# Block 2's gate and up in 512- and 256-column passes with its taps on ScalarE and GpSimd, and a fifth three-pass chunk in the first feed-forward

## The chip, the cores and the metric

The kernel runs on one core of a Trainium2 chip. The metric is the device time of one execution in microseconds (us). The engines are named as the profile names them: PE (TensorE, the matrix multiplier), PEld (its weight loads, which run beside the matmuls), DVE (VectorE), ACT (ScalarE), POOL (GpSimd) and SP (the engine that issues most of the loads). Every engine works through its own instructions in the order in which they were written; an instruction that waits holds up all that stand behind it on its engine.

## What is computed

A sequence of 256 positions by 1024 channels goes through two layers of a hybrid block (feed-forward, mixing of pooling and attention, feed-forward), and then through one layer of a second block ("block 2"), which ends in a feed-forward whose gate passes a causal convolution of three taps. Feed-forwards are five in all, each with 2816 hidden channels. All arithmetic is held to float32 accuracy.

```python
def swiglu(h, w_gate_up, w_down):             # the four of the two-layer block
    a, b = jnp.split(h @ w_gate_up, 2, axis=-1)
    return (jax.nn.silu(a) * b) @ w_down

def causal_dwconv(x, w, b):
    K = w.shape[0]
    S = x.shape[1]
    xp = jnp.pad(x, ((0, 0), (K - 1, 0), (0, 0)))
    y = xp[:, 0:S] * w[0]
    for k in range(1, K):
        y = y + xp[:, k:k + S] * w[k]
    return y + b
```

In block 2's feed-forward the gate is `gelu(causal_dwconv(h @ w_gate))` in place of the silu, and the layer's output is the sequence plus the down projection of gate times up. Ahead of every feed-forward stands a root-mean-square norm: each position is multiplied by its own factor (called RS here) and each channel by a gain.

## The kernel before

Channels lie on the 128 partitions and the 256 positions on the free axis, so the sequence `xT` is 8 tiles of 128x256. PE multiplies float32 numbers in a cut format, so every operand is split in a high part and a low one: ACT copies the raw weight to its high part (`wh`, line 86), DVE subtracts that from the raw weight and leaves the low part (`wl`, line 160); activations are split in the same way into the two halves of a tile `ahl`. Three products of the parts are summed: low by high, high by low, high by high.

A feed-forward has 22 hidden tiles, numbered k. Gate and up run in 11 chunks j of two hidden tiles each: a chunk is four column tiles (gate and up of k = 2j, then gate and up of k = 2j + 1), each with 8 weight tiles of 128x128, so 32 weight tiles a chunk. The down projection is 8 rows of 22 weight tiles. Two forms of the product are in use:

- **three-pass** (`cols`, `col_part`, `mm3`, lines 201 to 203): three matmuls of 256 columns for each weight tile. Its result lies in one half of a PSUM bank. The activations carry the gain and not RS, so the result is multiplied by RS when it is read.
- **wide** (`wide_cols`, `passes`, lines 247 and 252): for a group of weight tiles first a matmul of 512 columns each (the weight's high part against both halves of `ahl`), then one of 256 columns each (its low part against the high half). The result fills a whole bank, and DVE sums the two halves (`sum_halves`, line 255). Its activations carry gain and RS: `weigh` makes them, one call for each of the 8 tiles (DVE line 441, ACT line 86, POOL line 446, which subtracts the high part to leave the low one).

RS comes out of the norm's sums only while the first chunk is being multiplied, so a feed-forward begins in three-pass form. Each of the four silu feed-forwards runs three chunks so, the very first four (its first two in a form of their own, `opening`), makes the weighed activations in the last two of these, and runs the other chunks wide. Block 2's feed-forward (`gate is conv_gate`) runs all 11 chunks three-pass; it does not weigh anything and multiplies by RS on DVE where the gate is read (line 500) and where the down projection's result is read (line 457 in `add_to_x`). Down is wide in all five, but for its last row, which is three-pass.

After a column tile, `emit` or `halves` starts the gate, and `defer(n, f)` writes the later steps n ticks on; a tick is one group of matmuls. This, with `split` (which writes the weights' splits between ticks), fixes the order on every engine. The gate of block 2 (`conv_gate`) is an Identity with the third tap as scale and the bias (ACT, line 559), two taps by DVE (lines 562 and 563), and a Gelu (ACT, line 565). `finish` multiplies by up and splits the product for the down projection: copy on ACT (line 86, `ahl<-hh`), subtraction on POOL (line 512). Its multiplication is on POOL (line 513) in the silu feed-forwards, on DVE from PSUM in block 2. `silu_gate` is one ACT instruction (line 553). PSUM has four banks for these products, tag `mm`; the 128x256 work tiles share six buffers (`wt`), the larger activations 35 (`ut`).

Of the kernel before, what the change touches and what calls it, by code (L numbers as in the profile page):

```python
# [8 lines left out]
F = mybir.dt.float32  # L9
R = mybir.dt.float32r  # L10
AF = mybir.ActivationFunctionType
OP = mybir.AluOpType
AX = mybir.AxisListType

P = 128
S = 256
# [3 lines left out]
FT = DFF // P  # L20
# [25 lines left out]
def drain(gen, plan={}):  # L46

    for n, _ in enumerate(gen):
        if n in plan:
            plan[n]()  # L50
# [3 lines left out]
def tile_hybrid_stack(ctx, tc, wts, cst, prm, rows, small, out, x):  # L54
    nc = tc.nc
    pool = lambda name, bufs, **kw: ctx.enter_context(tc.tile_pool(name=name, bufs=bufs, **kw))
    cp = pool("consts", 1)
    wp = pool("weights", 4)
    up = pool("acts", 35)
    sp = pool("work", 2)  # L60
    mm = pool("mm", 4, space=bass.MemoryType.PSUM)
    tpp = pool("tp", 2, space=bass.MemoryType.PSUM)
# [5 lines left out]
        return up.tile(shape, dt, tag="u", name=name)  # L68

    def wt(name):  # L70
        return sp.tile([P, S], F, tag="w", name=name, bufs=6)

    def tiny(n, name, bufs=2):
        return sp.tile([P, n], F, tag=name, name=name, bufs=bufs)
# [10 lines left out]
    def copy(dst, src, **kw):  # L85
        nc.scalar.activation(dst, src, AF.Copy, **kw)  # L86
# [82 lines left out]
    def defer(steps, f):  # L169
        heapq.heappush(tasks, (now[0] + steps, next(order), f))  # L170
# [219 lines left out]
    RS = {}  # L390
# [58 lines left out]
    def add_to_x(norm, scale, rb=None):  # L449
        def emit(j, ps):  # L450
            if len(ps.shape) == 3 or rb is not None:
                d = wt("dx")
                if len(ps.shape) == 3:
                    sum_halves(d, ps)
                    ps = d
                if rb is not None:
                    nc.vector.tensor_tensor(d, ps, rb, OP.mult)
                ps = d
            nc.vector.scalar_tensor_tensor(xT[:, j], ps, scale, xT[:, j], op0=OP.mult, op1=OP.add)  # L459
            if norm is None:  # L460
                nc.sync.dma_start(out[:, j], xT[:, j])
            else:
                norm.done(j)
        return emit
# [25 lines left out]
    def feed_forward(norm, gate, nxt, scale, first=False, beside=None):  # L490


        hT = Acts(True)
        pace[0] = 2

        def emit(j):
            def f(i, pg, pu, both=None):
                k = 2 * j + i
                z, v = wt("sl"), wt("hh")
                nc.vector.tensor_tensor(z, pg, RS["bc"], OP.mult)  # L500
                if gate is not conv_gate:
                    nc.vector.tensor_tensor(v, pu, RS["bc"], OP.mult)
                a, n = gate(k, z)
                finish(k, v, a, n, pu if gate is conv_gate else v)
            return f

        def finish(k, v, a, n, src):
            eng = nc.gpsimd if src is v else nc.vector
            def last():
                dh, dl = hT.get(k)  # L510
                copy(dh, v)
                nc.gpsimd.tensor_tensor(dl, v, dh.bitcast(F), OP.subtract)  # L512
            defer(n, lambda: eng.tensor_tensor(v, src, a, OP.mult))  # L513
            defer(n + 1, last)

        def halves(j):

            gated = []

            def f(i, ps):  # L520
                k = 2 * j + i // 2
                z = wt("hh" if i % 2 else "sl")
                sum_halves(z, ps)
                if i % 2 == 0:
                    gated.append(gate(k, z))
                else:
                    a, n = gated.pop()
                    finish(k, z, a, max(n - 3, 1), z)
            return f
        if beside is not None:  # L530
            defer(60, beside)
        if first:
            opening(norm, emit(0), emit(1))
        done = 2 if first else 0
        if gate is conv_gate:
            last, factor = 11, RS
        else:
            last, factor = 4 if first else 3, {"bc": None}
        for j in range(done, last):
            plan = {}  # L540
            if last < 11 and j >= last - 2:
                steps = (0, 2, 4, 6) if j == last - 2 else (0, 1, 3, 4)
                plan = {m: lambda n=n: norm.weigh(4 * (j - last + 2) + n) for n, m in enumerate(steps)}
            drain(cols(norm.acts, KT, emit(j), None if j else norm), plan)
        pace[0], lead[0] = 1, 0
        for j in range(last, 11):
            drain(wide_cols(norm.weighed, halves(j)))
        flush()
        pace[0], lead[0] = 2, 1
        drain(wide_rows(hT, FT, *[add_to_x(nxt, scale, factor["bc"])] * 2))  # L550

    def silu_gate(f, z):
        defer(1, lambda: nc.scalar.activation(z, z, AF.Silu))
# [2 lines left out]
    def conv_gate(f, z):  # L556
        w = lambda k: pr[:, P_FCW + 3 * f + k:P_FCW + 3 * f + k + 1]
        a = wt("cz")
        nc.scalar.activation(a, z, AF.Identity, scale=w(2), bias=pr[:, P_FCB + f:P_FCB + f + 1])

        def rest():
            nc.vector.scalar_tensor_tensor(a[:, 1:], z[:, :S - 1], w(1), a[:, 1:], op0=OP.mult, op1=OP.add)
            nc.vector.scalar_tensor_tensor(a[:, 2:], z[:, :S - 2], w(0), a[:, 2:], op0=OP.mult, op1=OP.add)
        defer(1, rest)
        defer(2, lambda: nc.scalar.activation(a, a, AF.Gelu))
        return a, 3


    def rope_tables(col, rcol, n, name):
# [797 lines left out]
    norm = Norm(P_L, True)  # L1367
# [7 lines left out]
    for l in range(2):  # L1375
# [12 lines left out]
        norm = nxt  # L1388
# [140 lines left out]
```

## Time and profile before

| | before |
|---|---|
| time, median of 3 runs | 1494.89 us (1492.75 to 1497.18) |
| the profiled execution, its own time | 1496.27 us |
| its span | 1494.5 us |
| mean granted clock of PE | 0.995 of full speed |
| PE busy | 1466.1 us (98%), 10016 matmuls |
| DVE / ACT / POOL busy | 1043.8 / 772.8 / 442.3 us |

The span is the time from the first to the last instruction of the profiled execution; 1.8 us of its time lie around it. Shares of busy time are means over stages that differ. Where the chain of work runs through PE without a gap, only what PE does, or a new wait of PE, changes the time; where it leaves PE, the engine that it goes to counts. Block 2's feed-forward is at the end of the span, from about 1300 us on.

### The profile page before, as it was taken

How to read it: one execution, taken by the hardware profiler on the slowest of the kernel's cores; microseconds unless marked ns; L12 is line 12 of the kernel's file. 1: busy time of each engine (PE TensorE's matmuls, PEld its weight loads, DVE VectorE, ACT ScalarE, POOL GpSimd, SP SyncE). 2: the span in 40 equal slices, each digit the busy share in tenths (PEclk: the TensorE clock that was granted, in tenths of full speed). 3: DMA queues.
4: the chain of work that ended last, by engine and by line, in shares of the span. 5: the costliest groups of instructions: out<-in, count | busy, mean ns of one | idle time of the engine just before them, and what ended most of it. 6: DMA issues, size and time to landing. Idle time of an engine off the chain costs nothing.

```text
span 1494.5 us, 25193 instructions
## 1 busy us (share of the span) xinstructions
PE 1466.1 (98%) x10016; PEld 1351.9 (90%) x10016; DVE 1043.8 (70%) x1594; ACT 772.8 (52%) x1365; POOL 442.3 (30%) x513
## 2 busy tenths in 40 slices
PE   7999999999999999999999999999999799999998
PEld 7888888999988899888889999888987799999998
DVE  6867658577776757767586687676586666877673
ACT  4645335565554445544455645454376656555551
POOL 3642146013523135231360046322125101421200
PEclk9999999999999999999999999999999999999999
DMA  7555644445555544555443445546443533555561
GB/s 280 177 190 172 224 148 179 161 142 196 170 183 201 207 170 170 187 199 211 172 169 124 164 179 189 193 169 226 157 164 119 167 120 125 182 178 190 193 215 43
DMA packets 38710, 261.68 MB, mean 175 GB/s; under 512 B 4288, under 2 KB 5824, under 8 KB 7744
## 3 DMA queue, kind: packets, MB, share of 16 engines
q1 hardware_dynamic: 38016, 259.09, 49.5%
q8 instruction: 78, 1.28, 0.3%
q10 hardware_dynamic: 576, 0.98, 0.2%
q14 instruction: 40, 0.33, 0.1%
HBM read 259.01 MB, written 1.05 MB: 174 GB/s over the span
## 4 chain that ended last, share of the span: by engine, by line
PE 84%; DVE 8%; POOL 2%; ACT 2%; DMA 2%; issue 2%; SPq 0%; ACTq 0%; DVEq 0%; POOLq 0%
PE ps L247 27%; PE ps L252 14%; PE ps L201 13%; PE ps L202 13%; PE ps L203 13%; DVE wl L160 4%; DMA raw<-wts 2%; PE po L1226 1%; POOL rq L388 1%; ACT wh L86 1%; ACT ahl L86 0%; DVE ahl L413 0%; DVE y L441 0%; PE tp L610 0%; PE tp L1002 0%
## 5 line engine op out<-in xcount | busy, mean ns | idle before, releaser
L160 DVE TENSOR_TENSOR wl<-raw,wh 128x1024 fp32r<-128x1024 f32 (+2 forms) x661 | 652.9, 1023 | 143.8 <-ACT wh L86 142.7
L86 ACT ACTIVATE wh<-raw 128x1024 fp32r<-128x1024 f32 (+2 forms) x661 | 510.5, 823 | 54.1 <-DMA raw<-wts 27.3
L247 PE MATMUL ps<-ahl,wh 128*128 128x512 f32 x1762 | 443.7, 392 | 2.1 <-POOL ahl L446 2.1
L247 PEld LDWEIGHTS ps<-ahl,wh 128*128 128x128 f32 x1762 | 316.4, 189 | 59.1 <-POOL ahl L446 3.2
L252 PEld LDWEIGHTS ps<-ahl,wl 128*128 128x128 f32 x1762 | 241.5, 190 | 17.9
L201 PE MATMUL ps<-ahi,wl 128*128 128x256 f32 x864 | 253.2, 293 | 2.3 <-DVE wl L160 2.3
L201 PE MATMUL ps<-ahl,wl 128*128 128x256 f32 x846 | 242.5, 287 | 9.9 <-DVE wl L160 9.3
L252 PE MATMUL ps<-ahl,wl 128*128 128x256 f32 x1762 | 247.1, 282 | 0.0
L202 PE MATMUL ps<-alo,wh 128*128 128x256 f32 x864 | 245.5, 284 | 0.0
L203 PE MATMUL ps<-ahi,wh 128*128 128x256 f32 x864 | 245.3, 284 | 0.0
L202 PE MATMUL ps<-ahl,wh 128*128 128x256 f32 x846 | 240.4, 284 | 0.0
L203 PE MATMUL ps<-ahl,wh 128*128 128x256 f32 x846 | 240.2, 284 | 0.0
L201 PEld LDWEIGHTS ps<-ahi,wl 128*128 128x128 f32 x864 | 166.5, 193 | 9.3 <-DVE wl L160 4.3
L201 PEld LDWEIGHTS ps<-ahl,wl 128*128 128x128 f32 x846 | 163.3, 193 | 11.6 <-DVE wl L160 10.7
L202 PEld LDWEIGHTS ps<-alo,wh 128*128 128x128 f32 x864 | 166.7, 193 | 0.7 <-issue 0.5
L203 PEld LDWEIGHTS ps<-ahi,wh 128*128 128x128 f32 x864 | 166.6, 193 | 0.0
L202 PEld LDWEIGHTS ps<-ahl,wh 128*128 128x128 f32 x846 | 163.4, 193 | 0.1
L203 PEld LDWEIGHTS ps<-ahl,wh 128*128 128x128 f32 x846 | 163.4, 193 | 0.0
L513 POOL TENSOR_TENSOR hh<-hh,sl 128x256 f32<-128x256 f32 x88 | 81.5, 927 | 217.4 <-DVE hh L255 202.7
L512 POOL TENSOR_TENSOR ahl<-hh,ahl 128x256 fp32r<-128x256 f32 x110 | 99.3, 903 | 141.1 <-ACT ahl L86 136.6
L86 ACT ACTIVATE ahl<-hh 128x256 fp32r<-128x256 f32 x110 | 45.8, 416 | 155.8 <-POOL hh L513 134.0
L409 POOL TENSOR_TENSOR sq<-xT 128x256 f32<-128x256 f32 x56 | 36.2, 647 | 191.2 <-DVE xT L459 187.4
(269 smaller groups left out, 1504.8 us busy)
## 6 DMA issues: line engine op xcount, KB each, us to landing
raw<-wts SPq DMA_DIRECT2D x241, 1024.0 KB, 4.9
raw<-wts SPq DMA_DIRECT2D x2, 576.0 KB, 3.7
raw<-wts SPq DMA_DIRECT2D x4, 256.0 KB, 5.9
raw<-wts SPq DMA_DIRECT2D x2, 512.0 KB, 9.4
out_dram<-xT SPq DMA_DIRECT2D x8, 128.0 KB, 1.9
cs<-cst SPq DMA_DIRECT2D x1, 581.0 KB, 6.8
xT<-x SPq DMA_DIRECT2D x1, 512.0 KB, 8.4
pw<-pool_w ACTq DMA_DIRECT2D x2, 256.0 KB, 4.0
```

The source lines that it names most:

```text
L86: nc.scalar.activation(dst, src, AF.Copy, **kw)
L160: nc.vector.tensor_tensor(lo[:, c], raw[:, c], hi[:, c].bitcast(F), OP.subtract)
L201: nc.tensor.matmul(ps, ll, rh, start=start, stop=False)
L202: nc.tensor.matmul(ps, lh, rl, start=False, stop=False)
L203: nc.tensor.matmul(ps, lh, rh, start=False, stop=stop)
L247: nc.tensor.matmul(ps, wh, acts.both(k), start=k == 0, stop=False)
L252: nc.tensor.matmul(ps[:, 0], wl, acts.both(k)[:, 0], start=False, stop=k == nk - 1)
L388: nc.gpsimd.tensor_tensor(dst, src, half[:, :n], OP.pow)
L409: nc.gpsimd.tensor_tensor(sq, xT[:, j], xT[:, j], OP.mult)
L512: nc.gpsimd.tensor_tensor(dl, v, dh.bitcast(F), OP.subtract)
L513: defer(n, lambda: eng.tensor_tensor(v, src, a, OP.mult))
L1226: nc.tensor.matmul(po[t][b][:, h * 64:(h + 1) * 64], pT[:, b * (t + 1) + j], vn[:, j, b, g * 64:(g + 1) * 64], start=j == 0, stop=j == t)
```

## The change

Block 2's feed-forward takes the same form as the silu ones of the second layer: three three-pass chunks, the weighed activations made in its chunks 1 and 2, then eight wide chunks, and no RS in the down projection. Its two taps are no longer two DVE instructions: ACT makes two scaled copies of the gate (line 86), POOL adds them, shifted, in two instructions, and Gelu comes one tick later. Multiplication by up is on POOL for this gate as well. The very first feed-forward runs five chunks three-pass in place of four and weighs in its chunks 2 and 3, so that a chunk lies between the last weighing and the first wide chunk. The pool of larger activations has 34 buffers in place of 35, that of the work tiles 8 in place of 6.

```diff
-    up = pool("acts", 35)
+    up = pool("acts", 34)
...
-        return sp.tile([P, S], F, tag="w", name=name, bufs=6)
+        return sp.tile([P, S], F, tag="w", name=name, bufs=8)
...
                 nc.vector.tensor_tensor(z, pg, RS["bc"], OP.mult)
-                if gate is not conv_gate:
-                    nc.vector.tensor_tensor(v, pu, RS["bc"], OP.mult)
+                nc.vector.tensor_tensor(v, pu, RS["bc"], OP.mult)
                 a, n = gate(k, z)
-                finish(k, v, a, n, pu if gate is conv_gate else v)
+                finish(k, v, a, n)
...
-        def finish(k, v, a, n, src):
-            eng = nc.gpsimd if src is v else nc.vector
+        def finish(k, v, a, n):
             def last():
                 dh, dl = hT.get(k)
                 copy(dh, v)
                 nc.gpsimd.tensor_tensor(dl, v, dh.bitcast(F), OP.subtract)
-            defer(n, lambda: eng.tensor_tensor(v, src, a, OP.mult))
+            defer(n, lambda: nc.gpsimd.tensor_tensor(v, v, a, OP.mult))
             defer(n + 1, last)
...
-        if gate is conv_gate:
-            last, factor = 11, RS
-        else:
-            last, factor = 4 if first else 3, {"bc": None}
+        last = 5 if first else 3
+        weighing = (2, 3) if first else (1, 2)
         for j in range(done, last):
             plan = {}
-            if last < 11 and j >= last - 2:
-                steps = (0, 2, 4, 6) if j == last - 2 else (0, 1, 3, 4)
-                plan = {m: lambda n=n: norm.weigh(4 * (j - last + 2) + n) for n, m in enumerate(steps)}
+            if j in weighing:
+                steps = (0, 2, 4, 6) if j == weighing[0] else (0, 1, 3, 4)
+                plan = {m: lambda n=n: norm.weigh(4 * (j - weighing[0]) + n) for n, m in enumerate(steps)}
             drain(cols(norm.acts, KT, emit(j), None if j else norm), plan)
...
-        drain(wide_rows(hT, FT, *[add_to_x(nxt, scale, factor["bc"])] * 2))
+        drain(wide_rows(hT, FT, *[add_to_x(nxt, scale)] * 2))
...
         a = wt("cz")
         nc.scalar.activation(a, z, AF.Identity, scale=w(2), bias=pr[:, P_FCB + f:P_FCB + f + 1])
+        t1, t2 = wt("t1"), wt("t2")
+        copy(t1, z, scale=w(1))
+        copy(t2, z, scale=w(0))
+
         def rest():
-            nc.vector.scalar_tensor_tensor(a[:, 1:], z[:, :S - 1], w(1), a[:, 1:], op0=OP.mult, op1=OP.add)
-            nc.vector.scalar_tensor_tensor(a[:, 2:], z[:, :S - 2], w(0), a[:, 2:], op0=OP.mult, op1=OP.add)
+            for d, t in ((1, t1), (2, t2)):
+                nc.gpsimd.tensor_tensor(a[:, d:], a[:, d:], t[:, :S - d], OP.add)
         defer(1, rest)
-        defer(2, lambda: nc.scalar.activation(a, a, AF.Gelu))
-        return a, 3
+        defer(3, lambda: nc.scalar.activation(a, a, AF.Gelu))
+        return a, 4
```

The order of the instructions differs in two places alone: in the very first feed-forward's fifth chunk, and in block 2's feed-forward. On SP it is the same throughout. A row below names an instruction's line, operation, output and inputs, and the output's size; of the changed kernel the Identity is line 555, the taps' additions line 563, the Gelu line 565, the multiplication by up line 511, the subtraction behind it line 510. `cz` is the tile that collects the convolution, `t_...` a tap's copy, `sl` the gate and `hh` up as read from PSUM.

ACT in the middle of block 2's gate and up, before: the Identity and the Gelu of a hidden tile, then its copy to `ahl`, with the weights' copies in whole pieces between them.

```order
L559 ACTIVATE cz<-sl,pr 128x256
L86 ACTIVATE wh<-raw 128x1024
L565 ACTIVATE cz<-cz 128x256
L86 ACTIVATE ahl<-hh 128x256
L559 ACTIVATE cz<-sl,pr 128x256
L565 ACTIVATE cz<-cz 128x256
L86 ACTIVATE wh<-raw 128x1024 x2
```

ACT of the changed kernel there, one wide chunk, from the gate of an odd hidden tile to the gate of the next odd one.

```order
L555 ACTIVATE cz<-sl,pr 128x256
L86 ACTIVATE t_14830<-sl,pr 128x256
L86 ACTIVATE t_14831<-sl,pr 128x256
L565 ACTIVATE cz<-cz 128x256
L86 ACTIVATE ahl<-hh 128x256
L86 ACTIVATE wh<-raw 128x1024 x2
L555 ACTIVATE cz<-sl,pr 128x256
L86 ACTIVATE t_14886<-sl,pr 128x256
L86 ACTIVATE t_14887<-sl,pr 128x256
L86 ACTIVATE wh<-raw 128x512 x2
L565 ACTIVATE cz<-cz 128x256
L86 ACTIVATE wh<-raw 128x512 x2
```

Two copies stand behind each Identity, and the weights' two large copies stand behind the copy `ahl<-hh` of the odd hidden tile, with nothing between its Gelu and that copy.

DVE at the same place of the changed kernel, from the sum of an odd hidden tile's gate to the sum of the next even tile's up.

```order
L255 TENSOR_REDUCE sl<-ps 128x256
L255 TENSOR_REDUCE hh<-ps 128x256
L160 TENSOR_TENSOR wl<-raw,wh 128x1024
L255 TENSOR_REDUCE sl<-ps 128x256
L160 TENSOR_TENSOR wl<-raw,wh 128x1024
L160 TENSOR_TENSOR wl<-raw,wh 128x512 x2
L255 TENSOR_REDUCE hh<-ps 128x256
L160 TENSOR_TENSOR wl<-raw,wh 128x512 x2
```

Where DVE had two taps for each hidden tile before (lines 562 and 563), it has sums of halves now, and the sum of an even tile's gate stands behind the weights' low part that the first of the two large copies on ACT releases.

POOL at the start of block 2's feed-forward in the changed kernel, from the first taps to the first weighed activations; before, there were only the subtractions of line 512 here, 22 in the whole feed-forward.

```order
L563 TENSOR_TENSOR cz<-cz,t_13740 128x255
L563 TENSOR_TENSOR cz<-cz,t_13741 128x254
L563 TENSOR_TENSOR cz<-cz,t_13776 128x255
L563 TENSOR_TENSOR cz<-cz,t_13777 128x254
L511 TENSOR_TENSOR hh<-hh,cz 128x256
L510 TENSOR_TENSOR ahl<-hh,ahl 128x256
L446 TENSOR_TENSOR ahl<-y,ahl 128x256
L511 TENSOR_TENSOR hh<-hh,cz 128x256
L510 TENSOR_TENSOR ahl<-hh,ahl 128x256
L446 TENSOR_TENSOR ahl<-y,ahl 128x256
```

Up to the last of the eight weighings (line 446) 26 instructions stand on POOL now; in a silu feed-forward of the second layer's form 18 stand up to there.

## Rows read from the trace of the kernel before

**Rows 1.** The page: busy us, share of the span and instructions.

```profile
PE 1466.1 (98%) x10016; PEld 1351.9 (90%) x10016; DVE 1043.8 (70%) x1594; ACT 772.8 (52%) x1365; POOL 442.3 (30%) x513
```

**Rows 2.** Windows, block 2: length, busy PE, PEld, DVE, ACT, POOL, clock, DMA, GB/s.

```profile
1315.00:1420.00 105.00, 105.00 (x878) 105.00 (x877) 74.61 (x111) 60.47 (x95) 22.34 (x19) 1.00 0.54 182
```

**Rows 3.** The longest of PE's waits over the span: total us, times, longest one.

```profile
PE ps L201 <- DVE wl L160: 11.6, 10, 7.5
```

**Rows 4.** Timeline of PE, block 2: start, us, instruction; third passes, 54 matmuls apart.

```profile
1400.05 0.28 PE L203 MATMUL ps<-ahl,wh 128*128 128x256 f32 x1
...
1406.53 0.28 PE L203 MATMUL ps<-ahl,wh 128*128 128x256 f32 x1
```

**Rows 5.** Timeline of PE, wide chunks of the first feed-forward.

```profile
100.22 2.00 PE L247 MATMUL ps<-ahl,wh 128*128 128x512 f32 x8
...
103.01 2.00 PE L247 MATMUL ps<-ahl,wh 128*128 128x512 f32 x8
```

**Rows 6.** Timeline of PE, first wide chunk of all; idle time in brackets.

```profile
63.85 0.50 PE L247 MATMUL ps<-ahl,wh 128*128 128x512 f32 x1 [0.77 <-POOL ahl L446]
65.41 0.50 PE L247 MATMUL ps<-ahl,wh 128*128 128x512 f32 x1 [1.06 <-POOL ahl L446]
```

**Rows 7.** Timeline, the end of the span.

```profile
1490.53 0.42 DVE L457 TENSOR_TENSOR dx<-ps,rbc 128x256 f32<-128x256 f32 x1 [6.30 <-PE ps L203]
1490.99 0.42 DVE L459 SCALAR_TENSOR_TENSOR xT<-dx,xT 128x256 f32<-128x256 f32 x1
```

**Rows 8.** Timelines of PE and POOL, second feed-forward, its first wide matmuls.

```profile
394.50 2.00 PE L247 MATMUL ps<-ahl,wh 128*128 128x512 f32 x8
...
371.50 0.74 POOL L513 TENSOR_TENSOR hh<-hh,sl 128x256 f32<-128x256 f32 x1 [4.02 <-ACT sl L553]
...
394.73 0.74 POOL L446 TENSOR_TENSOR ahl<-y,ahl 128x256 fp32r<-128x256 f32 x1
```

**Rows 9.** Timeline of DVE, one wide chunk of the second feed-forward.

```profile
415.40 0.68 DVE L255 TENSOR_REDUCE sl<-ps 128x256 f32<-128x512 f32 x1
417.11 0.69 DVE L255 TENSOR_REDUCE hh<-ps 128x256 f32<-128x512 f32 x1 [1.03 <-PE ps L252]
420.12 1.23 DVE L160 TENSOR_TENSOR wl<-raw,wh 128x1024 fp32r<-128x1024 f32 x1 [2.31 <-ACT wh L86]
421.26 0.69 DVE L255 TENSOR_REDUCE sl<-ps 128x256 f32<-128x512 f32 x1
```

**Rows 10.** Timelines of POOL and ACT, the same chunk.

```profile
417.95 0.74 POOL L513 TENSOR_TENSOR hh<-hh,sl 128x256 f32<-128x256 f32 x1 [1.75 <-DVE hh L255]
...
418.72 0.42 ACT L86 ACTIVATE ahl<-hh 128x256 fp32r<-128x256 f32 x1 [2.13 <-POOL hh L513]
419.04 1.99 ACT L86 ACTIVATE wh<-raw 128x1024 fp32r<-128x1024 f32 x2
```

**Rows 11.** Windows, the same chunk, columns as in rows 2.

```profile
416.86:428.04 11.18, 11.18 (x67) 9.84 (x66) 7.83 (x10) 5.66 (x10) 3.27 (x4) 1.00 0.54 185
```

**Rows 12.** Groups by form, 1300 to 1430: busy us, mean ns, idle before.

```profile
L559 ACT ACTIVATE cz<-sl,pr 128x256 f32<-128x256 f32 x22 | 13.2, 601 | 14.4 <-DVE sl L500 14.4
L86 ACT ACTIVATE wh<-raw 128x512 fp32r<-128x512 f32 x4 | 2.3, 616 | 0.0
L562 DVE SCALAR_TENSOR_TENSOR cz<-sl,pr,cz 128x255 f32<-128x255 f32 x22 | 10.7, 487 | 14.2 <-ACT cz L559 14.1
```

**Rows 13.** Timelines of DVE and POOL, the second feed-forward, two instructions at once.

```profile
378.65 3.44 DVE L160 TENSOR_TENSOR wl<-raw,wh 128x1024 fp32r<-128x1024 f32 x2
...
379.29 1.72 POOL L513 TENSOR_TENSOR hh<-hh,sl 128x256 f32<-128x256 f32 x1
```

**Rows 14.** Timelines of DVE, POOL and PE, second feed-forward, gate and up's end.

```profile
482.44 0.68 DVE L255 TENSOR_REDUCE sl<-ps 128x256 f32<-128x512 f32 x1
...
486.25 0.74 POOL L512 TENSOR_TENSOR ahl<-hh,ahl 128x256 fp32r<-128x256 f32 x1 [0.53 <-ACT ahl L86]
...
489.47 1.55 PE L247 MATMUL ps<-ahl,wh 128*128 128x512 f32 x6
```

More of the change, by code (lines that the diff above doesn't have):

```diff
@@ L527, in f @@
                     a, n = gated.pop()
-                    finish(k, z, a, max(n - 3, 1), z)
+                    finish(k, z, a, max(n - 3, 1))
             return f
```

## The prediction

> **What bounds the kernel now.** I read the page first: PE is busy for 1466.1 of the 1494.5 us [rows 1]. The windows over block 2's gate and up say the same more sharply: 105.00 us of PE in 105.00 [rows 2], while DVE works 74.61, ACT 60.47 and POOL 22.34 of them. PE's waits have one large line in the whole span, 11.6 us for weights' low parts [rows 3], none of it in that stretch. So there is nothing to win there but PE's own work, and whatever the other engines do better there is worth nothing. Then I read the timeline of PE for what a weight tile costs in each form, the second feed-forward for how a feed-forward of the new form runs with a silu gate, and last its DVE, ACT and POOL for what such a chunk would be with the new gate.
>
> **The change part by part: what it saves.** A three-pass tile is three matmuls; 54 of them, 18 tiles, lie 6.48 us apart [rows 4], so 0.120 a matmul and 0.360 us a tile, 11.52 a chunk of 32. A wide column tile of 8 takes 103.01 - 100.22 = 2.79 us [rows 5], and a whole wide chunk 11.18 [rows 11]. Eight chunks save 8 x 0.34 = 2.7 us. The first feed-forward's fifth chunk is three-pass now and costs 0.34; for that a chunk's time lies between the last weighing and its reader, and the two waits of 0.77 and 1.06 go [rows 6]: a gain of 1.83 - 0.34 = 1.5. At the very end the multiplication by RS falls away: 1490.99 - 1490.53 = 0.46 [rows 7]. Together 4.7 us.
>
> DVE's taps, 22 times two instructions of about 0.49 [rows 12], leave an engine that idles 30 of 105 us while PE idles none [rows 2]: worth nothing as they stand. The multiplication of up by RS, six times 0.42 in the three-pass chunks, lies in the same idle time; if that cover were gone it would be 2.5. The smaller pool of activations I cost at nothing: in a feed-forward at most 22 products and 8 weighed tiles are live at once, 30 of 34. The eight work tiles cover five for each hidden tile (gate, up, `cz`, two copies), so a tile is taken again behind a reader that stands earlier in the same order; nothing, too. In both the other end is a wait of one hidden tile, 5.6 us [rows 11], once; a gain is excluded, since PE waits for neither.
>
> **What it costs: the chain in a wide chunk.** The order of ACT and DVE shows a ring. From the sum of an odd hidden tile's gate on DVE the way is: Identity and two copies (ACT), two additions (POOL), Gelu (ACT), multiplication (POOL), copy `ahl<-hh` (ACT), and only behind it, in ACT's queue, the next large weight copy; behind that the large `wl` on DVE; and behind that, in DVE's queue, the sum of the next even tile's gate. None can start before the one ahead ends.
>
> First half. The sum takes 0.68 [rows 9], the hand-over I put at 0.10, the Identity 0.60 [rows 12], the first copy 0.42 as the other activations of that size [rows 10] (no row shows a scaled copy between work tiles; the bounds are that and the Identity's 0.60, which takes the same operands): 1.80. The additions are not in the trace on POOL; its two-input instruction of that size takes 0.74 [rows 10] and DVE's 0.49 [rows 12]. I take 0.74, less some overlap, since it is the same engine: with hand-overs 3.30. The Gelu, 0.42 with the hand-over 0.03 to 0.07, brings the multiplication's start to 3.82. From there the rest is read straight from a silu chunk, where the same instructions follow each other: multiplication at 417.95, copy 418.72, weights 419.04 [rows 10], `wl` 420.12, next gate's sum 421.26 [rows 9], so 3.31. First half: 7.1 us.
>
> Second half, from the even gate's sum to the odd one's. Sum, hand-over, Identity and both copies (0.68 + 0.10 + 0.60 + 2 x 0.42, less 0.09 of overlap) end at 2.13, the first small weight copy (0.62 [rows 12]) at 2.75; then DVE has four small `wl` and up's sum, 0.6 each (half of the large one's 1.14, from 420.12 to 421.26 [rows 9], and the sum's 0.68 less overlap): 5.8. Two of the small `wl` meet POOL's additions. Where a `wl` and a multiplication on POOL ran together, the `wl` took 3.44 / 2 = 1.72 in place of 1.23, and POOL 1.72 in place of 0.74 [rows 13]. So twice 0.49 more: 6.8 us.
>
> The ring is 13.9 us; PE needs 11.18 [rows 11]. Seven rounds lie between the first odd gate of the wide chunks and the last, and one second half (6.8 against 5.6) before: 7 x 2.7 + 1.2 = 20.2 us. Without any meeting of DVE and POOL a round is 12.9 and the term 12.3; with one POOL instruction a round lengthened by 1.0 as in [rows 13] a round is 14.9 and the term 27. In the silu chunk the ring is shorter than PE's work: up's sum there waits for PE, 1.03 [rows 9].
>
> The Trainium skill, "GPSIMD Engine Reference", § 4.1 Engine selection, gives elementwise work with two inputs to VectorE and calls GpSimd about two times slower at it; this speaks against the taps' new place. By that rule an addition would be an estimated 0.97, twice the DVE tap, a round 14.8 and the sum 6.4 us higher; the row of POOL shows 0.74, 1.5 times, and decides. Its § 8 Key points says that GpSimd shares its SBUF interfaces with VectorE when that has two SBUF inputs; the trace agrees, 1.23 to 1.72.
>
> **What it costs: the head and the end.** In the second feed-forward 18 POOL instructions stand up to the last weighing, from 371.50 to 395.47 [rows 8]; the first wide group needs it at its eighth matmul, near 396.1 (eight in 2.00 us), 0.6 later. In block 2 there are 26: eight taps more, at 0.74, make the last weighing 5.9 later and PE wait 5.2. Bounds: nothing, if they all fell in POOL's 6.5 us without work in that stretch, and 8 x 0.97 = 7.8, the mean of those 18 (17.5 us busy), many of them lengthened. At the end, from the last gate's sum to the low part of the last product, a silu gate needs 4.55 (482.44 to 486.99 [rows 14]); here 3.82 and the 2.0 from multiplication to low part, 1.3 more. Against that, the silu feed-forward ends that part at 486.99 and PE reads it at its sixth matmul, near 490.6 [rows 14]: 3.6 us to spare.
>
> **Sum.** 5.2 + 20.2 + 1.3 - 3.6 = 23.1 us of new waits; less 4.7 it is 18.4 slower. On the profiled execution's 1496.27 us that is 1514.7; the median of the runs lies 1.4 lower, so 1513.3. With the low ends (0, 12.3) the loss is 5.3, with the high ones (7.8, 27) 27.8: 1500 to 1523. Were PE's clock, 1.00 in [rows 2], to fall in its waits, the longer matmuls would lie in the 2.7 us that each round leaves free.
>
> **The rivals.** *All hidden, faster.* Counted by busy time, no engine but PE is full: a wide chunk has DVE 7.83, ACT 5.66 and POOL 3.27 [rows 11]; the change adds two copies and a longer gate for each of two hidden tiles (2 x 1.4 on ACT), four additions on POOL (3.0), and meetings on DVE (about 2), so 9.8, 8.5 and 6.3 of 11.18. If the engines ran so far ahead of PE that the ring never closed, only the 4.7 would remain: 1490.2. It decides at a ring of 11.18. The order speaks against it: the ring is closed by two queues, not by PE. The skill's "Perfetto Trace Analysis", § Identifying the Most-Contended Engine, finds the bottleneck by occupancy; by that rule this rival would come true, and the rows of before, with PE full, agree with it.
>
> *Only the head waits, no change.* If the ring is no longer than PE's chunk, as when hand-overs and meetings are less than I put them, the eight extra taps ahead of the last weighing stay: -4.7 + 5.2, 1495.4. For it speaks that a silu chunk has 1.03 of DVE waiting for PE [rows 9]; against it that a silu chunk's halves, 5.86 from 415.40 to 421.26 and the other 5.32 of 11.18 [rows 9, 11], grow by 1.3 and 1.5 with the new gate, by the terms above.
>
> *The change does as it says and POOL is the bound.* With each POOL instruction lengthened to 1.72 a chunk's eight would be 13.8, as long as the ring; that is inside the forecast's upper bound.
>
> **How the numbers follow.** Forecast 0.76, all hidden 0.13, head alone 0.11. A measurement of this kernel can tell about 0.3%, 4.5 us, from no change. The forecast is slower from end to end. All hidden is 4.7 faster, near that line: 0.09 faster, 0.04 same. Head alone is the same. Faster 0.09, same 0.15, slower 0.76. The range leaves out all hidden, half of head alone and the forecast's last microsecond: 1495.5 to 1522. The forecast's own is 1500 to 1523.
>
> **What the profile after would show.** In block 2's wide chunks a window of one period is near 13.9, not 11.18, with PE busy some 11.2 in it and waiting for DVE (`wl` or the sums); Gelu waits for POOL; the sum of an even gate starts as its `wl` ends. The first wide matmul of block 2 waits about 5 for POOL's weighing. The waits of [rows 6] are gone. If the period is 11.18 the ring was wrong; if the wait is at the end of gate and up alone, the slack was; if PE waits elsewhere, a buffer was.

## The result and the profile after

| | before | changed |
|---|---|---|
| median | 1494.87 us (4 runs, 1492.75 to 1497.18) | 1515.98 us (4 runs, 1515.52 to 1516.64) |
| span of the profiled execution | 1494.5 us | 1513.7 us |

The ratio is 1.0142, with a 95% interval of 1.013 to 1.0154: 21.1 us slower, where the forecast was 18.4.

The windows of the changed kernel, one round of the wide chunks in block 2 (length, busy PE, PEld, DVE, ACT, POOL, clock, DMA, GB/s), against [rows 2] and [rows 11]:

```profile
1390.26:1404.01 13.75, 12.47 (x67) 9.79 (x66) 8.22 (x11) 8.45 (x16) 6.01 (x9) 1.00 0.44 151
```

A chunk takes 13.75 us where PE has 11.18 to do, and no engine is full. (PE's 12.47 counts matmuls held up while they wait for their weights: six wide ones at 1400.14 take 2.06, and 1.55 in [rows 14].) Why the chunk is long is read from the timelines of that round, first DVE, then ACT, then POOL:

```profile
1391.40 0.68 DVE L255 TENSOR_REDUCE sl<-ps 128x256 f32<-128x512 f32 x1
1392.00 0.68 DVE L255 TENSOR_REDUCE hh<-ps 128x256 f32<-128x512 f32 x1
1397.34 1.23 DVE L160 TENSOR_TENSOR wl<-raw,wh 128x1024 fp32r<-128x1024 f32 x1 [4.67 <-ACT wh L86]
1398.49 0.68 DVE L255 TENSOR_REDUCE sl<-ps 128x256 f32<-128x512 f32 x1
1399.09 1.21 DVE L160 TENSOR_TENSOR wl<-raw,wh 128x1024 fp32r<-128x1024 f32 x1
1401.16 1.73 DVE L160 TENSOR_TENSOR wl<-raw,wh 128x512 fp32r<-128x512 f32 x2 [0.86 <-ACT wh L86]
1402.81 0.68 DVE L255 TENSOR_REDUCE hh<-ps 128x256 f32<-128x512 f32 x1
1403.41 1.82 DVE L160 TENSOR_TENSOR wl<-raw,wh 128x512 fp32r<-128x512 f32 x2
1405.16 0.68 DVE L255 TENSOR_REDUCE sl<-ps 128x256 f32<-128x512 f32 x1
...
1392.11 0.60 ACT L555 ACTIVATE cz<-sl,pr 128x256 f32<-128x256 f32 x1 [0.73 <-DVE sl L255]
1392.62 0.89 ACT L86 ACTIVATE t<-sl,pr 128x256 f32<-128x256 f32 x2
1394.68 0.42 ACT L565 ACTIVATE cz<-cz 128x256 f32<-128x256 f32 x1 [1.16 <-POOL cz L563]
1395.94 0.42 ACT L86 ACTIVATE ahl<-hh 128x256 fp32r<-128x256 f32 x1 [0.85 <-POOL hh L511]
1396.27 1.99 ACT L86 ACTIVATE wh<-raw 128x1024 fp32r<-128x1024 f32 x2
...
1393.19 1.45 POOL L563 TENSOR_TENSOR cz<-cz,t 128x255 f32<-128x255 f32 x2 [1.00 <-ACT t L86]
1395.17 0.74 POOL L511 TENSOR_TENSOR hh<-hh,cz 128x256 f32<-128x256 f32 x1 [0.53 <-ACT cz L565]
```

Read by start time, the rows are one line of handovers: sum 1391.40, Identity 1392.11, copies 1392.62, additions 1393.19, Gelu 1394.68, multiplication 1395.17, copy 1395.94, weights 1396.27, their low part 1397.34, and the next even gate's sum 1398.49. DVE stood still for 4.67 us in the middle of it, although PE had ended the tile of that sum at 1394.7 (the last of its rows starts at 1393.61 and takes 1.11). The first half of a round, from this odd gate's sum to the even one's, is 7.09 us; the second, on to the next odd gate's sum at 1405.16, is 6.67.

PE's waits over the whole span (total, times, longest), of which [rows 3] has the line that was there before:

```profile
PE ps L201 <- DVE wl L160: 11.9, 11, 7.3
PE ps L247 <- POOL ahl L446: 5.6, 3, 5.0
PE ps L247 <- POOL ahl L510: 3.9, 1, 3.9
PE ps L252 <- DVE wl L160: 3.4, 5, 0.7
PE ps L247 <- ACT wh L86: 2.8, 5, 0.6
```

The timeline of PE where these two long waits stand, the first wide chunk of block 2 and the end of its gate and up:

```profile
1338.06 1.48 PE L247 MATMUL ps<-ahl,wh 128*128 128x512 f32 x2 [4.98 <-POOL ahl L446]
...
1341.05 2.53 PE L247 MATMUL ps<-ahl,wh 128*128 128x512 f32 x8
...
1452.19 0.79 PE L247 MATMUL ps<-ahl,wh 128*128 128x512 f32 x1 [3.89 <-POOL ahl L510]
...
1454.07 3.61 PE L247 MATMUL ps<-ahl,wh 128*128 128x512 f32 x8
```

Behind both waits the matmuls are slow: eight wide ones take 2.53 and 3.61 where [rows 5] have 2.00. The windows there show the granted clock at 0.50, the lower of its two levels:

```profile
1338.00:1340.00 2.00, 1.94 (x6) 1.45 (x7) 0.08 (x1) 1.83 (x5) 1.47 (x4) 0.50 0.88 369
1454.00:1456.00 2.00, 2.00 (x7) 1.61 (x6) 2.00 (x3) 2.00 (x4) 0.00 (x0) 0.50 0.43 70
```

What was to be gained is there. The first wide matmuls of all follow without a wait, against [rows 6], and behind the last matmul DVE has one instruction where it had two, against [rows 7]:

```profile
72.74 2.00 PE L247 MATMUL ps<-ahl,wh 128*128 128x512 f32 x8
...
1510.20 0.42 DVE L459 SCALAR_TENSOR_TENSOR xT<-ps,xT 128x256 f32<-128x256 f32 x1 [6.70 <-PE ps L203]
```

### The profile page after: what moved, and what is told of

It is laid out like the page before. It is cut to its first block, busy times and chain, and to the rows that moved or that the text cites. A ratio compares the mean times of both kernels' runs of the same rounds, so it can differ in the third digit from the quotient of the medians.

```text
span 1513.7 us, 24926 instructions
## 1 busy us (share of the span) xinstructions
PE 1473.7 (97%) x9792; PEld 1340.7 (89%) x9792; DVE 1041.4 (69%) x1564; ACT 794.5 (52%) x1431; POOL 492.8 (33%) x587
## 4 chain that ended last, share of the span: by engine, by line
PE 78%; DVE 9%; POOL 4%; ACT 4%; issue 3%; DMA 1%; SPq 0%; POOLq 0%; DVEq 0%; ACTq 0%
PE ps L247 28%; PE ps L252 14%; PE ps L201 11%; PE ps L202 10%; PE ps L203 10%; DVE wl L160 5%; POOL cz L563 1%; DMA raw<-wts 1%; ACT wh L86 1%; PE po L1226 1%; POOL hh L511 1%; POOL rq L388 1%; ACT ahl L86 0%; PE tp L1002 0%; PE at L1209 0%
## 5 line engine op out<-in xcount | busy, mean ns | idle before, releaser
L160 DVE TENSOR_TENSOR wl<-raw,wh 128x512 fp32r<-128x512 f32 (+2 forms) x675 | 665.2, 1019 | 197.9 <-ACT wh L86 195.2
L86 ACT ACTIVATE wh<-raw 128x512 fp32r<-128x512 f32 (+2 forms) x675 | 512.1, 809 | 56.0 <-PE ps L247 19.7
L247 PE MATMUL ps<-ahl,wh 128*128 128x512 f32 x1986 | 508.7, 395 | 12.5 <-POOL ahl L446 5.6
L247 PEld LDWEIGHTS ps<-ahl,wh 128*128 128x128 f32 x1986 | 358.4, 190 | 84.0 <-ACT wh L86 9.6
L252 PEld LDWEIGHTS ps<-ahl,wl 128*128 128x128 f32 x1986 | 274.5, 192 | 24.9 <-DVE wl L160 4.7
L252 PE MATMUL ps<-ahl,wl 128*128 128x256 f32 x1986 | 281.6, 284 | 3.5 <-DVE wl L160 3.4
L201 PE MATMUL ps<-ahl,wl 128*128 128x256 f32 x622 | 178.9, 288 | 9.9 <-DVE wl L160 9.6
L202 PE MATMUL ps<-ahl,wh 128*128 128x256 f32 x622 | 176.6, 284 | 0.0
L203 PE MATMUL ps<-ahl,wh 128*128 128x256 f32 x622 | 176.5, 284 | 0.0
L201 PEld LDWEIGHTS ps<-ahl,wl 128*128 128x128 f32 x622 | 119.9, 193 | 11.8 <-DVE wl L160 11.3
L202 PEld LDWEIGHTS ps<-ahl,wh 128*128 128x128 f32 x622 | 120.0, 193 | 0.1
L203 PEld LDWEIGHTS ps<-ahl,wh 128*128 128x128 f32 x622 | 120.0, 193 | 0.0
L510 POOL TENSOR_TENSOR ahl<-hh,ahl 128x256 fp32r<-128x256 f32 x110 | 92.7, 844 | 57.2 <-ACT ahl L86 56.6
L409 POOL TENSOR_TENSOR sq<-xT 128x256 f32<-128x256 f32 x56 | 37.7, 673 | 192.3 <-DVE xT L459 187.1
```

Source lines behind the costliest of these rows:

```text
L160: nc.vector.tensor_tensor(lo[:, c], raw[:, c], hi[:, c].bitcast(F), OP.subtract)
L201: nc.tensor.matmul(ps, ll, rh, start=start, stop=False)
L202: nc.tensor.matmul(ps, lh, rl, start=False, stop=False)
L203: nc.tensor.matmul(ps, lh, rh, start=False, stop=stop)
L247: nc.tensor.matmul(ps, wh, acts.both(k), start=k == 0, stop=False)
L252: nc.tensor.matmul(ps[:, 0], wl, acts.both(k)[:, 0], start=False, stop=k == nk - 1)
```

## The experiments

The theory was that of the prediction: a ring through the queues of DVE and ACT, with POOL's instructions on the way. The rival was that POOL's additions and their meetings with DVE make the chunk long, or ACT's added work, in whatever order.

**The buffers alone**, on the kernel before.

```diff
-    up = pool("acts", 35)
+    up = pool("acts", 34)
-        return sp.tile([P, S], F, tag="w", name=name, bufs=6)
+        return sp.tile([P, S], F, tag="w", name=name, bufs=8)
```

> The kernel before with 34 larger buffers and 8 work tiles, nothing else. In the changed kernel the stages whose order did not change ended 3.5 us sooner than in the profiled execution of before (mixing of block 2: 2.1 and 1.3). Theory 1, that is how executions of before differ among themselves (its runs lie 4.4 us apart): 1494.9 as before, within 0.15%. Rival: the buffers free a wait there: about 3.5 less, 1491.4.

Measured: 1494.51 us, ratio 1.0008 (0.9999 to 1.0017). The buffers gain nothing, and cost 2.5 us at most.

**The first feed-forward alone**: `last = 5 if first else 3`, with the weighing in chunks 2 and 3, on the kernel before.

> The kernel before with only the fifth three-pass chunk in the first feed-forward. The prediction: two waits of 1.83 go, 0.34 is added: 1.5 less, 1493.4. The trace of the changed kernel has this feed-forward 2.3 shorter by the start of the second: 1492.6. If nothing of that stays: 1494.9.

Measured: 1492.18 us, 1493.69 of before beside it; ratio 0.9985 (0.9976 to 0.9994). The medians lie 1.5 apart, the ratio says 2.2 (0.9 to 3.6): the term of 1.5 fits.

**Gelu late.** The changed kernel with three more ticks to Gelu in the wide chunks.

```diff
-        defer(3, lambda: nc.scalar.activation(a, a, AF.Gelu))
-        return a, 4
+        m = 6 if pace[0] == 1 else 3
+        defer(m, lambda: nc.scalar.activation(a, a, AF.Gelu))
+        return a, m + 1
```

> The changed kernel, but in the wide chunks of block 2 Gelu and what follows it are written three ticks later, so that on ACT the next large weight copy stands ahead of the odd tile's Gelu. No work is added or removed. Theory, the ring through two queues: it is open now, a round falls from 13.75 to PE's 11.2, and the wait at the end of gate and up with the slow matmuls behind it goes; only the head's wait stays: about 1495 to 1497, 19 to 21 less. Rival, the meetings of POOL and DVE and the added work (ACT 8.45, DVE 8.2, POOL 6.0 in a round) make the round long: the same work meets, so the round stays over 13 and the time over 1511.

Measured: 1503.85 us, ratio 1.0064 (1.0047 to 1.008), 12 less than the change; a round is 12.15. Nothing but the order differs, so the order costs those 12. The theory's number was missed. The timeline of DVE shows what was left:

```profile
1391.49 1.62 DVE L160 TENSOR_TENSOR wl<-raw,wh 128x1024 fp32r<-128x1024 f32 x1 [2.13 <-ACT wh L86]
1393.03 0.68 DVE L255 TENSOR_REDUCE sl<-ps 128x256 f32<-128x512 f32 x1
1393.63 1.21 DVE L160 TENSOR_TENSOR wl<-raw,wh 128x1024 fp32r<-128x1024 f32 x1
1395.70 2.28 DVE L160 TENSOR_TENSOR wl<-raw,wh 128x512 fp32r<-128x512 f32 x2 [0.86 <-ACT wh L86]
1397.90 0.68 DVE L255 TENSOR_REDUCE hh<-ps 128x256 f32<-128x512 f32 x1
```

The first half fell from 7.09 to 4.95. The second grew to 7.20: two small low parts now take 2.28 beside POOL in place of 1.73. The meetings have a share of their own. A small low part takes 0.68 where it meets nothing; in the changed kernel's round two of the four take 1.13 and 1.22, so about 1.0 of the 13.75 is meetings, as forecast in size (one meets the additions, the other the multiplication). Here three take 1.13 to 1.23, and a large one 1.62 in place of 1.23, about 1.9 of the 12.15. That is enough to keep this round above 11.18, but more meetings and a shorter round cannot make the meetings the cause of the 13.75.

**DVE taps in the changed kernel**: `conv_gate` as before, no copies, no additions on POOL; everything else as changed.

> The changed kernel, but the two taps on DVE as before, no copies on ACT and no additions on POOL; Gelu one tick sooner as before. Theory, the ring: its first half is 0.8 shorter (6.25), its second about as long (6.6 to 7.0), a round 12.8 to 13.2, 4 to 7 us less over seven rounds; and with 18 POOL instructions up to the last weighing the head's wait goes (5.4, and about 3 of slow matmuls with it): about 1500 to 1504. Rival, the additions on POOL and their meetings with DVE are what lengthens the round: with no additions the round is PE's 11.2, about 1489 to 1491.

Measured: 1511.2 us, ratio 1.0118 (1.0104 to 1.0132); a round is 13.50, halves 6.48 and 7.02. Both expectations missed, the rival's by 20, the theory's by 7 or more. With no addition on POOL a round is only 0.25 shorter, so additions and meetings on POOL are not what the round needs to be long. What they cost by themselves this run does not say: DVE has the taps in its queue again (9.64 busy in a round against 8.22), and Gelu stands a tick sooner. And the head kept a wait of 4.2 us for the weighings (3.3 the longest) with 17 POOL instructions up to the last one in place of 26, which the prediction's head term can't explain.

**The copy late.** The changed kernel; in the wide chunks `ahl<-hh` and the subtraction behind it two ticks later.

```diff
-            defer(n + 1, last)
+            defer(n + (3 if gate is conv_gate and pace[0] == 1 else 1), last)
```

> The changed kernel, but in the wide chunks of block 2 only the copy to ahl and the subtraction behind it are written two ticks later, so that on ACT the large weight copies of the next chunk stand behind the odd tile's Gelu and no longer behind its multiplication and copy. Theory, the ring: its first half loses the multiplication and the copy (7.08 to about 5.9), its second gains one activation copy ahead of the small weight copies (6.67 to about 7.0), a round of about 12.9 in place of 13.75: 5 to 7 us less than the changed kernel, about 1510. Rival, meetings of POOL and DVE: the same instructions meet, 1516.

Measured: 1525.1 us, ratio 1.0196 (1.018 to 1.0211), a round 14.96. Slower by 9, where the theory said faster by 6. Timelines of ACT and POOL:

```profile
1397.92 0.89 ACT L86 ACTIVATE t<-sl,pr 128x256 f32<-128x256 f32 x2
1398.72 0.40 ACT L86 ACTIVATE ahl<-hh 128x256 fp32r<-128x256 f32 x1
1401.37 0.42 ACT L565 ACTIVATE cz<-cz 128x256 f32<-128x256 f32 x1 [2.25 <-POOL cz L563]
...
1399.20 0.74 POOL L510 TENSOR_TENSOR ahl<-hh,ahl 128x256 fp32r<-128x256 f32 x1 [3.57 <-ACT ahl L86]
1399.89 1.45 POOL L563 TENSOR_TENSOR cz<-cz,t 128x255 f32<-128x255 f32 x2
```

The copy did leave the path to the weights. But on POOL the subtraction of the tile before stands ahead of the new tile's additions. It stood there in the changed kernel too, where its copy came early enough (subtraction 1391.46, additions 1393.19); here it waits for the late copy, and the first addition begins at 1399.89, about 1.6 after the first tap was copied. The first half keeps its length by that (7.21), and the second, where the small weight copies now wait behind such a Gelu, grows from 6.67 to 7.74. There is a third queue in the ring, POOL's, and the theory of two was too small. (The rival, 1516, missed too.)

**A fourth three-pass chunk** in block 2 of the changed kernel, nothing weighed in it: `last = 4` for this gate.

> The changed kernel with a fourth three-pass chunk in block 2, so that a chunk lies between the last weighing and the first wide matmul that needs it. The prediction's head term: the wait of 5.4 goes, with the slow matmuls behind it the first even gate's sum is no longer 8.4 late; and with seven wide chunks there is one round less (2.6); against that 0.34 for the chunk: 10 to 11 us less than the changed kernel, about 1505. Rival: the three-pass chunks of block 2 have a ring of their own that is longer than their 11.5 of PE, so that lateness goes on through the fourth: 0 to 4 less, 1512 to 1516.

Measured: 1515.01 us, ratio 1.0133 (1.012 to 1.0147): the rival. The wait for the weighings is gone, and PE waits 3.3 us in the three-pass chunks instead, for weights' low parts, the longest 1.9. The lateness goes on through the fourth chunk: the first even gate's sum of the wide chunks comes 50.9 behind RS's spread, 13.1 later than in the change, for 11.52 more of work.

**All 11 chunks three-pass with the new taps**: `last = 11` for this gate, nothing weighed.

> The changed kernel with all 11 chunks of block 2 three-pass as before, nothing weighed; taps, multiplication by up and buffers as in the change, RS at up and not in the down projection. Theory: the new taps cost nothing where the weights' low parts do not stand between a hidden tile's chain and the next tile's sum; a round is PE's 11.52, and the time is that of the fifth chunk in the first feed-forward alone less the multiplication at the end, 1492.2 - 0.5 = 1491.7. Rival, the taps on ACT and POOL are by themselves too slow for PE's pace: over 1495.

Measured: 1505.39 us, ratio 1.0073 (1.006 to 1.0085); a chunk takes 13.01. The rival was right in the time. Timelines of ACT, POOL and DVE in one chunk:

```profile
1373.94 0.40 ACT L86 ACTIVATE ahl<-hh 128x256 fp32r<-128x256 f32 x1
...
1374.42 0.74 POOL L510 TENSOR_TENSOR ahl<-hh,ahl 128x256 fp32r<-128x256 f32 x1 [0.86 <-ACT ahl L86]
1375.12 2.31 POOL L563 TENSOR_TENSOR cz<-cz,t 128x255 f32<-128x255 f32 x2
...
1377.46 0.42 ACT L565 ACTIVATE cz<-cz 128x256 f32<-128x256 f32 x1 [2.17 <-POOL cz L563]
1377.79 1.99 ACT L86 ACTIVATE wh<-raw 128x1024 fp32r<-128x1024 f32 x2
...
1378.87 1.23 DVE L160 TENSOR_TENSOR wl<-raw,wh 128x1024 fp32r<-128x1024 f32 x1 [1.93 <-ACT wh L86]
1380.01 0.42 DVE L500 TENSOR_TENSOR sl<-ps,rbc 128x256 f32<-128x256 f32 x1
```

It is the same picture: copy, subtraction of the old tile, additions of the new one, Gelu, weights, low part, sum. Two causes could stand behind it, POOL's order or the additions themselves, 2.31 beside a low part on DVE. A later run bears on it.

**The ring opened.** The changed kernel with `m = 6` in the wide chunks as above, the copy one tick later there, the weights in whole pieces (`pace[0]` 2), and four three-pass chunks.

> The changed kernel with the ring opened on both sides and the head mended: in block 2's wide chunks Gelu and multiplication three ticks later and the copy behind them one more, the weights split in whole large pieces (no small ones), and a fourth three-pass chunk. Theory: first half 4.95 as with Gelu late alone, second about 6.1 (two large weight copies behind the even gate's copies, their low parts, up's sum), 11.05 in all, so PE's 11.18 bounds: seven wide chunks save 2.4, the end 0.5, the first feed-forward 1.5 of its own run against before: 1489.3, under both kernels. Rival, meetings of POOL and DVE lengthen the large low parts to 1.6 or more each: a round near 12, 1495 or more.

Measured: 1495.26 us, 1494.78 of before beside it; ratio 1.0001 (0.9992 to 1.001), 20.7 less than the change. Two sums of one kind follow each other in 10.94, less than PE's 11.18, and from the third wide chunk on PE waits for nothing until the end, as a window over one chunk shows:

```profile
1424.10:1435.28 11.18, 11.18 (x66) 9.84 (x65) 5.98 (x8) 6.57 (x14) 7.24 (x10) 1.00 0.55 188
```

The time is the rival's, the round is not. So the ring in the wide chunks was the cause there: once it is opened, by order and by whole weight pieces, the meetings don't keep PE from its pace. The forecast gain is missing, and the waits that are left stand in the three-pass chunks and in the first two wide ones:

```profile
PE ps L201 <- DVE wl L160: 3.3, 3, 1.9
PE ps L247 <- ACT wh L86: 1.4, 2, 1.1
```

**Taps by form**: the same with DVE taps in the three-pass chunks.

> The kernel with the ring opened (Gelu and the copy late, whole weight pieces, a fourth three-pass chunk), but with the taps on DVE as before in the three-pass chunks, and on ACT and POOL in the wide chunks alone. Theory: what kept the kernel with the ring opened from gaining is the same ring in its three-pass chunks (waits of 3.3 for low parts, 1.3 at the first wide chunk, slow matmuls behind them); with DVE taps these chunks keep PE's pace, and the wide ones do as they did (a round of 10.9, under PE's 11.2): the gains of 2.4, 0.5 and 1.5 to 2 stay, 1490.2. Rival: the weighings delay the head by themselves, also with DVE taps, and the wait of 2 to 4 with slow matmuls stays: 1494 or more.

Measured: 1492.3 us, 1495.04 of before beside it; ratio 0.9982 (0.9973 to 0.9991). In between: the wide chunks run without any wait of PE, but the last 314 matmuls before them take 41.6 us against 37.7 at 0.120 each; PE idles 1.8 of it, and the granted clock is 0.96 over that window.

**The subtraction late**: all 11 chunks three-pass with the new taps, one number different from the run above whose chunk took 13.01. The copy on ACT and the subtraction on POOL move together, by one tick.

```diff
-            defer(n + 1, last)
+            defer(n + (2 if gate is conv_gate else 1), last)
```

> All 11 chunks three-pass with the new taps, but the copy to ahl and the subtraction on POOL one tick later, so that on POOL a tile's additions stand ahead of the subtraction of the tile before, and not behind it. Theory, the ring has POOL's queue in it too: the additions no longer wait for the copy (which stands on ACT behind the new tile's Identity and copies) and for the subtraction, 8.3 of a round's 13.0 becomes about 6.9, a round 11.6, which is about PE's 11.52: 1492 to 1496. Rival, the additions by themselves (2.3 beside the low parts on DVE) are too long: a round of 12.5 to 13, 1501 to 1505.

Measured: 1489.02 us, 1495.04 of before beside it; ratio 0.9965 (0.9954 to 0.9976), 16.4 less than with the other order. Timeline of POOL, and the window that answers to [rows 2]:

```profile
1377.14 1.47 POOL L563 TENSOR_TENSOR cz<-cz,t 128x255 f32<-128x255 f32 x2 [1.12 <-ACT t L86]
1378.55 0.74 POOL L510 TENSOR_TENSOR ahl<-hh,ahl 128x256 fp32r<-128x256 f32 x1
...
1315.00:1420.00 105.00, 105.00 (x877) 105.00 (x876) 65.55 (x73) 72.33 (x129) 69.49 (x75) 1.00 0.54 184
```

The additions are first, the subtraction second, and PE is full again with POOL at 69 of 105 us: the same additions don't hold PE up, so the rival falls and the third queue is shown. They also start where they meet no low part, 1.47 in place of 2.31; the new order makes them start about 1.4 sooner behind the copies and last 0.8 less, and no run separates the two. This kernel is faster than the one before and than the change, with the first feed-forward's fifth chunk and no wide chunk in block 2.

**Both together, the weighings spread** over three of five three-pass chunks (3, 3, 2), then six opened wide chunks; first with the new taps and the late subtraction, then with DVE taps in the three-pass chunks.

> Five three-pass chunks in block 2 with the new taps and the subtraction late, the eight weighings spread over three of them (3, 3, 2), then six wide chunks with the ring opened (Gelu late, copy later, whole weight pieces). Theory: three-pass rounds stay at PE's 11.52 as with 11 such chunks (1489.0, before 1495.0 beside it), wide ones at 11.18: 6 x 0.34 = 2.0 less, 1487.0 against 1495.0. Rival: the weighings still make PE wait 2 to 3 in the three-pass chunks and its clock falls behind the wait, 1490 to 1493.

> As the run beside it, but with DVE taps in the five three-pass chunks. Theory: with eight weighings in three chunks in place of two the wait of 1.8 and the slow matmuls behind it (4 us in all with four chunks) go: 1487 to 1488. Rival: DVE has both the taps and the weighings in these chunks and PE waits as before, 1491 to 1493.

Measured: 1490.18 us, ratio 0.9967 (0.9957 to 0.9977), and 1491.54, ratio 0.998 (0.9972 to 0.9989), with 1494.99 of before beside both. The rivals: 1.7 us of waits, or 1.2, are left in the three-pass chunks. The 2 us that six wide chunks save go there.

## Why the prediction was right, and where not

**The ring was right in place, kind and size.** Forecast 7.1 + 6.8 = 13.9, measured 7.09 + 6.67 = 13.75. Taking the second half of the first from a silu chunk, where the same instructions stand, held within 0.1. Gelu late shows that the order of the same work makes most of the difference, and the ring opened that PE's pace comes back. What the prediction left out is that POOL's queue can close it as well; in the changed kernel's wide chunks it did not (additions 1393.19, right behind the copies), in its three-pass chunks it did.

**The head term was right in size and wrong in its cause.** Forecast a wait of 5.2, measured 4.98 and 0.42. But eight more instructions on POOL is not what it is: with DVE taps there are 17 in place of 26 and the wait is 4.2; with a fourth chunk it moved to the three-pass matmuls, and the total fell by 1.0. The size was luck. The step that failed is the one that took the three-pass chunks as hidden behind PE, when weighings and the new gate's chain together run longer than their 11.52. In the changed kernel DVE reads the odd gates of chunks 1 and 2 15.3 apart, and PE, which ran through these chunks without a wait, meets the lateness at the first wide one:

```profile
1322.09 0.41 DVE L500 TENSOR_TENSOR sl<-ps,rbc 128x256 f32<-128x256 f32 x1
...
1337.34 0.41 DVE L500 TENSOR_TENSOR sl<-ps,rbc 128x256 f32<-128x256 f32 x1
```

The same two reads lie 12.6 apart with the new taps and nothing weighed (13.0 in later chunks), and 11.52 with the subtraction late as well. So with the new taps the weighings and POOL's order both have a part. With DVE taps the reads lie 13.8 apart, and it is DVE that has taps, `y` and low parts in one queue; that part is read from waits, no run took it apart.

**The end term** held: from the last gate's sum, 1446.41, to the end of the last subtraction, 1452.14, it is 5.7 (forecast 5.8), and PE waited.

**The clock was missed.** The prediction let it hide in the rounds. Behind the two long waits it does not: from the read of the last product (1452.19) to the end of the wide part of down (1501.97) it is 49.8 us, in the second feed-forward 46.9, so 2.8 more; and the first even gate's sum in the wide chunks is 8.4 later than there, where the wait is 5.4.

**The sum.** From the matmul behind RS's spread in block 2's feed-forward to the last of its down projection, the profiled executions have 179.85 (1310.36 to 1490.21) and 205.39 (1304.50 to 1509.89): 25.5 more. Forecast 23.1 - 2.7 = 20.4 for it; the clock's 2.8 and the head's further lateness (8.4 against the 5.2), less 1.0 of rings that are a little shorter, are the difference. The rest of the span is 6.3 shorter: 0.5 at the end, 2.3 by the start of the second feed-forward (1.5 forecast), and 3.5 in block 2's mixing, whose order is unchanged. Some 2.1 of that belong to the execution and not to the change: from the spread of RS there (line 431) to the transposes of line 1002 ahead of line 1257 it is 108.6 in the profiled execution of before, 106.5 in that of the change, and 106.5 to 108.7 in those of the experiments without regard to the edit. The rest lies behind a wait of PE, first before, then changed:

```profile
PE tph L1257 <- ACT pT L86: 2.9, 1, 2.9
...
PE tph L1257 <- ACT pT L86: 0.7, 1, 0.7
```

ACT had stood there for a load of weights, 2.37 us in the kernel before and 2.34 with the buffers alone, where PE's wait is 2.9 too. In the profiled executions of all kernels with the first feed-forward's fifth chunk ACT stood 0.2 at most, and PE 0.4 to 0.8; from those transposes to the next spread of RS it is 117.8 and 119.0 without that chunk, 116.3 to 116.7 with it. So this part may be the fifth chunk's, which the prediction did not have; why the load comes sooner no run shows. That the total came so near is in part luck, errors of opposite sign.

**All hidden** failed as foreseen: by busy time a round had 8.45 of ACT and 8.22 of DVE in 13.75, and no occupancy showed the bound. The Trainium skill's "Perfetto Trace Analysis", § Identifying the Most-Contended Engine, takes the engine with the highest occupancy, with weight loads as the measure for PE, and would have pointed to PE here (PEld 9.79); this trace doesn't agree, since PE's 11.18 of work is not what set the 13.75. **Head alone** failed with it. POOL's additions took 0.73 each where they met nothing (1.45 for two), and 1.16 beside a low part (2.31). By the rule of the Trainium skill's "GPSIMD Engine Reference", § 4.1 Engine selection, it was an estimated 0.97; the rows lie on both sides of it.

What stays open: the fastest kernel is 0.9965 of before, the first feed-forward's change alone 0.9985, and between the two only the multiplication at the end (0.5 us, 0.0003) is known to be saved; their block 2 feed-forwards are equally long, 179.85 and 179.86. The rest, some 2.5 us by the ratios, lies in stages that both have alike, and their intervals touch.

## What to carry to other kernels

Where engines work their queues in order, follow one tile's chain through the queues and write down what stands behind each of its steps: if the way leads back to the next tile's first step, its length is a bound that no busy share shows. Open it by order before moving work: three ticks were worth 12 us, one tick 16. A step that is moved takes its place in another queue, and what stands behind it there must be followed too; the copy that was moved here cost 9 us that way.

## What was not expected of the hardware

After waits of PE of 4.98 and 3.89 us the granted clock was 0.50, the lower level, for some 4 and 6 us; in the rounds, with waits of 0.56 and 0.68 and PE busy 12.47 of 13.75, it was 1.00. Two low parts of 128x512 on DVE took 2.28 beside POOL's additions and subtraction and 1.41 in the run with the copy late, where POOL worked for a short part of them; the sums out of PSUM took 0.68 in every one of these rounds.
